# Attention stages of an encoder trunk in another order between its projections: a query tile every four projection steps, first stages begun fewer steps behind their projection

## The chip, the cores and the metric

The kernel runs on one core of a Trainium2 chip. The core has a matrix engine (TensorE, PE in the profile, with its weight loads as PEld), a vector engine (DVE), a scalar engine (ACT), GpSimd (POOL) and a queue that issues the DMAs (SyncE, SP). Each engine works through its own instructions in a fixed order and waits on semaphores for the others. The metric is the device time of one execution in microseconds (us); lower is better. Several executions are timed, and one more is taken with a profile.

## The reference

Two layers of an encoder on 512 tokens of width 1024, all in float32. One layer:

```
h = RMSNorm(x);  z = h @ W_in          # one wide projection, cut into parts
a = DifferentialAttention(z)           # 4 heads; per head two softmaxes p0, p1 over all 512 keys
b = DilatedWindowAttention(z)          # 3 groups x 8 heads, masked windows, joined by denominators
m = (sigmoid(gA) * (a @ W_a) + sigmoid(gB) * (b @ W_b)) @ W_out
x = x + RMSNorm(m);  x = x + RMSNorm(SwiGLU(RMSNorm(x)))
```

Differential attention, per head, with 128-wide values, is

```
s_c = q_c k_c^T / 8;  p_c = softmax(s_c) for c = 0, 1
a = p_0 - lam * p_1;  o = RMSNorm(a @ v) * (1 - lambda_init)
```

Queries and keys pass a rotary embedding (rope) first.

## The kernel before

**Split numbers.** Each large product takes three matmuls: both operands are split into a high and a low part, and high·high, high·low and low·high are added (`mm3`, lines 117 to 123). The high part of a weight is cast on ACT (L106 or L109), the low part is the difference, on DVE (L107 or L110). Rotated queries and keys of differential attention, and of the first dilated group, are split in the same way (L458 on ACT, L459 on DVE).

**Projections are cut into steps.** `ws_gen` (line 191) yields after every 12 matmuls of 128x512, and the value projection `proj_v` yields after 24 of 128x256. Such a stretch of PE work is called a projection step here. `drive` (line 183) runs a projection and calls `att_step` after each step. One layer has 104 steps: 4 for the first half of differential attention (u = 0; its queries and keys were projected earlier), 12 for its second half (u = 1), 72 for the six dilated groups (u = 0, 1; gi = 0, 1, 2) with 12 each, and 16 for gates.

**Attention is a queue of jobs.** `att_push` (line 164) appends a job with the step at which it is due: the clock plus an entry of `DELAY`. `att_step` (line 167) advances the job at the head of the queue by one step, and the job behind it too once the head "drains", that is, once it has begun its last query tile's scores and one period has passed. Thus a job starts when it is due or when the one ahead drains, whichever is later. What the stages of a step issue on PE stands between two projection steps. When the projections end, a loop (`while attq`) empties the queue.

**A job of differential attention** (`da_attn`, line 478) handles two heads and four query tiles of 128 rows. Each tile has four stages: *scores* (24 small matmuls, L484, into four PSUM tiles `at0` to `at3`; then for each head two maxima on DVE, L490, two exponentials on ACT, L492, a reciprocal and two combinations on DVE, L496, L498, L500), *turn* (four PE transposes per head, L510, into `at0` and `at1`, copied out by ACT, L512), *values* (16 matmuls, L519, into `at4`; then squares on ACT, L525, and the norm on DVE and POOL, ending in L530) and *finish* (two transposes, L537, into the upper half of the same `at4`, read by ACT, L540, and DVE, L541). `pipeline` (line 546) sets at which step of the job each stage of each tile runs: stage lag plus period times tile. Before, the period is 3 and the lags are 0, 2, 4 and 6.

**A job of a dilated group** (`g_attn`, line 571) has scores (L583), a masked softmax (L591, L593, L596), a turn (16 transposes, L610, into `at0` to `at3`, copied by DVE, L611) and values (L626 or L629, into `at4`), with a period of 4. Group 0 has two blocks of queries, the others one. **The join** of the three groups (`combine`, line 650) does vector work, lets five steps pass, and then turns its result in two parts (L679, both in `at4`, read by ACT, L682, and DVE, L683).

**Who orders what.** PE's instructions go in the order in which the program writes them. The instructions of the other engines and the DMAs on SP are put in order ahead of the run by a planner, by priority and expected readiness; the splits of weights have a raised priority (`SPLIT_PRI`). Each engine then keeps that order. The buffers of the attention are few: one PSUM tile for each of `at0` to `at4`, three for projections (`pj`), eight tiles `e` for exponentials and what is made of them.

## Time and profile before

| what | value |
|---|---|
| median of 3 runs | 1914.05 us (1913.56 to 1915.93) |
| the profiled execution's own time | 1916.6 us |
| its span, first to last instruction | 1914.8 us |
| PE busy | 1847.7 us, 10720 matmuls |
| DVE busy | 917.0 us |
| ACT busy | 659.3 us |
| POOL busy | 183.0 us |
| mean granted clock of PE | 0.988 |

The profile gives the busy time of each engine, groups of instructions by source line with the idle time before them and who ended it, and the same for stretches of time. A row such as "PE at L510 <- DVE e L500: 9.4, 6, 2.9" reads: PE, at line 510 with output `at`, waited for DVE's line 500 with output `e`; 9.4 us in all, 6 times, 2.9 us the longest. In a row of the timeline, the first number is the start in us from the span's start, the second the duration, and a bracket holds the idle time of the engine just before and what ended it. In a table by stretches, each engine's busy time is followed by its number of instructions; PEclk is the granted clock of PE as a share of full speed. Differential attention lies at about 77 to 215 us in the first layer and 1020 to 1160 us in the second.

### The profile page before, as it was taken

What the parts mean: (1) busy time and instruction counts of PE and PEld (TensorE: products, weight loads), DVE (VectorE), ACT (ScalarE), POOL (GpSimd) and SP (SyncE); (2) the same over time, 40 slices, a digit from 0 to 9 for tenths busy, and PEclk for the clock granted to TensorE, in tenths of its full rate; (3) what the DMA queues carried; (4) which work ended last, traced back from release to release, by engine and by line L of the source; (5) the groups of instructions that cost most, each with busy time, mean ns of one, the idle gap of its engine ahead of it and who ended that gap; (6) DMA issues with size and microseconds to landing.
All of it is one profiled execution on the core that took longest, in us unless ns stands there. A gap on an engine that the chain in (4) does not pass through costs nothing. (4 is left out here: it accounts for less than half of the span.)

```text
span 1914.8 us, 25447 instructions
## 1 busy us (share of the span) xinstructions
PE 1847.7 (96%) x10720; PEld 1579.5 (82%) x10720; DVE 917.0 (48%) x1243; ACT 659.3 (34%) x1273; POOL 183.0 (10%) x132
## 2 busy tenths in 40 slices
PE   6998999999999999999999889999999999999997
PEld 6887888987888888888888779989878888888886
DVE  4565658644446333332455666584443543333222
ACT  3354434443224222221333544333432342222221
POOL 1211113110100000000011111221110000000000
PEclk9998999999999999999999999999999999999999
DMA  6312223222245322323432212232224433232232
GB/s 184 97 45 75 67 90 113 73 88 87 90 150 169 110 88 97 101 88 109 144 115 81 82 45 71 86 117 76 82 88 141 145 111 110 88 102 97 88 121 66
DMA packets 148066, 190.45 MB, mean 99 GB/s; under 512 B 7536, under 2 KB 132848, under 8 KB 147952
## 3 DMA queue, kind: packets, MB, share of 16 engines
q1 hardware_dynamic: 147952, 188.83, 30.8%
q8 instruction: 84, 1.38, 0.3%
q14 instruction: 30, 0.25, 0.0%
HBM read 176.16 MB, written 12.65 MB: 99 GB/s over the span
## 5 line engine op out<-in xcount | busy, mean ns | idle before, releaser
L121 PE MATMUL pj<-hTh,whi 128*128 128x512 f32 (+1 forms) x1536 | 588.7, 383 | 2.5 <-ACT hTh L246 2.5
L122 PE MATMUL pj<-hTl,whi 128*128 128x512 f32 (+1 forms) x1536 | 582.0, 379 | 5.9 <-DVE hTl L247 5.9
L123 PE MATMUL pj<-hTh,wlo 128*128 128x512 f32 (+1 forms) x1536 | 580.7, 378 | 0.0
L107 DVE TENSOR_TENSOR wlo<-raw,whi 128x1024 fp32r<-128x1024 f32 x252 | 338.8, 1345 | 500.5 <-ACT whi L106 500.3
L106 ACT CAST whi<-raw 128x1024 fp32r<-128x1024 f32 x252 | 264.7, 1051 | 772.2 <-PE pj L122 527.5
L121 PEld LDWEIGHTS pj<-hTh,whi 128*128 128x128 f32 x1536 | 292.4, 190 | 60.3 <-ACT hTh L246 4.7
L122 PEld LDWEIGHTS pj<-hTl,whi 128*128 128x128 f32 x1536 | 292.4, 190 | 57.4 <-DVE hTl L247 7.4
L123 PEld LDWEIGHTS pj<-hTh,wlo 128*128 128x128 f32 x1536 | 292.2, 190 | 53.6
L121 PE MATMUL pj<-whi,hTh 128*128 128x256 f32 x512 | 150.3, 294 | 0.0
L122 PE MATMUL pj<-wlo,hTh 128*128 128x256 f32 x512 | 147.2, 288 | 0.0
L123 PE MATMUL pj<-whi,hTl 128*128 128x256 f32 x512 | 147.1, 287 | 0.0
L75 POOL TENSOR_TENSOR sm<-sm,mhalf 128x1 f32<-128x1 f32 (+1 forms) x48 | 30.6, 637 | 1010.0 <-DVE sm L73 1010.0
L121 PEld LDWEIGHTS pj<-whi,hTh 128*128 128x128 f32 x512 | 100.6, 197 | 3.4 <-issue 2.7
L596 ACT ACTIVATE e<-e,gst 128x128 f32<-128x128 f32 (+1 forms) x192 | 81.3, 425 | 58.8 <-DVE gst L593 58.8
L122 PEld LDWEIGHTS pj<-wlo,hTh 128*128 128x128 f32 x512 | 100.8, 197 | 0.2
L123 PEld LDWEIGHTS pj<-whi,hTl 128*128 128x128 f32 x512 | 100.6, 196 | 0.0
L794 DVE TENSOR_TENSOR s<-s,pj 128x512 f32<-128x512 f32 x42 | 28.9, 688 | 123.6 <-PE pj L123 123.6
L285 PE MATMUL at<-whi,ac 128*128 128x512 f32 x200 | 78.8, 394 | 0.0
L284 PE MATMUL at<-whi,ac 128*128 128x512 f32 x200 | 78.5, 392 | 0.0
L286 PE MATMUL at<-wlo,ac 128*128 128x512 f32 x200 | 77.7, 389 | 0.0
L492 ACT ACTIVATE e<-at,sm 128x512 f32<-128x512 f32 x64 | 43.7, 685 | 55.7 <-DVE sm L490 55.7
L110 DVE SCALAR_TENSOR_TENSOR wlo<-raw,whi 128x1024 fp32r<-128x1024 f32 x32 | 48.0, 1503 | 15.6 <-ACT whi L109 15.3
(174 smaller groups left out, 2391.2 us busy)
## 6 DMA issues: line engine op xcount, KB each, us to landing
raw<-in_w_in_dram SPq DMA_DIRECT2D x64, 1024.0 KB, 5.7
raw<-in_w_gate_up_dram SPq DMA_DIRECT2D x44, 1024.0 KB, 5.0
raw<-in_w_down_dram SPq DMA_DIRECT2D x22, 1024.0 KB, 4.9
raw<-in_w_out_dram SPq DMA_DIRECT2D x8, 1024.0 KB, 4.9
xs<-m SPq DMA_DIRECT2D x12, 512.0 KB, 2.9
m<-xs SPq DMA_DIRECT2D x12, 512.0 KB, 5.6
m<-in_x_dram SPq DMA_DIRECT2D x32, 128.0 KB, 5.4
raw<-in_w_a_dram SPq DMA_DIRECT2D x8, 512.0 KB, 3.5
```

Source lines behind the costliest of these rows:

```text
L75: nc.gpsimd.tensor_tensor(out=r, in0=t, in1=mhalf[:, 0:n], op=ALU.pow)
L106: nc.scalar.copy(out=shp(hi), in_=src)
L107: nc.vector.tensor_tensor(out=shp(lo), in0=src, in1=shp(hi.bitcast(F32)), op=ALU.subtract)
L110: nc.vector.scalar_tensor_tensor(out=shp(lo), in0=src, scalar=scale, in1=shp(hi.bitcast(F32)), op0=ALU.mult, op1=ALU.subtract)
L121: nc.tensor.matmul(o, ah, bh, start=(i == 0), stop=False)
L122: nc.tensor.matmul(o, ah, bl, start=False, stop=False)
L123: nc.tensor.matmul(o, al, bh, start=False, stop=(i == n - 1))
L284: nc.tensor.matmul(o, ah, hi[:, sl], start=(k == 0), stop=False)
L285: nc.tensor.matmul(o, al, hi[:, sl], start=False, stop=False)
L286: nc.tensor.matmul(o, ah, lo[:, sl], start=False, stop=(k == nk - 1))
L492: nc.scalar.activation(out=e, in_=oc, func=AF.Exp, bias=nmx[:, c:c + 1], accum_out=den[:, c:c + 1])
L596: nc.scalar.activation(out=e[:, i, :], in_=e[:, i, :], func=AF.Exp, bias=sts[:, n, h:h + 1], accum_out=sts[:, n, 4 + h:5 + h])
```

## The change

```diff
-DELAY = (4, 4, 2, 2, 3)
+DELAY = (1, 3, 1, 1, 2)
...
-            yield from pipeline(NT, 3, ((finish, 6), (values, 4), (turn, 2), (scores, 0)))
+            yield from pipeline(NT, 4, ((turn, 3), (finish, 7), (values, 5), (scores, 0)))
...
             for pr in range(2):
                 yield True
+                yield True
                 tp = at(4, (P, 4, P))
```

No computation is added or removed; only the places of the stages between the projection steps change. `DELAY` holds, in order, the delays of differential attention, of dilated groups 0, 1 and 2, and what is added for u = 0 of differential attention. So the job of u = 0 is due 3 steps after its projection and not 7, that of u = 1 after 1 and not 4, and the groups after 3, 1 and 1 steps and not 4, 2 and 2. Within a job of differential attention a tile's scores come every 4 steps and not every 3. A tile's turn follows its scores 3 steps later and not 2; values follow the turn after 2 steps and finish follows values after 2 steps, as before. In the step that holds a turn and the previous tile's finish, the turn now stands first. In `combine`, one more step passes ahead of each of the two turns.

## Prediction

> **What bounds the kernel now.** I read the page first, then PE's waits, then the stretches around them, then single rows. The page's busy times say that PE is the bound.

> ```profile
> PE 1847.7 (96%) x10720; PEld 1579.5 (82%) x10720; DVE 917.0 (48%) x1243; ACT 659.3 (34%) x1273; POOL 183.0 (10%) x132
> ```

> Of the span of 1914.8 us PE is idle for 67.1, and an order alone can win only from that, and from what the clock loses. PE's waits say where in attention the idle time lies (line, who ended it: us in all, times, longest).

> ```profile
> PE at L510 <- DVE e L500: 9.4, 6, 2.9
> PE at L519 <- DVE big L541: 9.4, 4, 3.7
> PE at L510 <- ACT e L492: 8.5, 4, 2.2
> PE at L679 <- DVE big L683: 4.6, 2, 2.3
> PE at L510 <- DVE sm L73: 2.6, 4, 0.8
> ```

> L510 is the turn: it waits 20.5 us for the softmax of its own tile. L519 is values: it waits for the readers of the last finish, which share `at4`. Both belong to differential attention. L679 is the second turn of the join. The stretches of differential attention, one for each layer, and inside the first one those after long waits:

> ```profile
> 77.00:215.00 138.00, 122.89 (x869) 104.02 (x868) 87.44 (x171) 62.39 (x155) 21.56 (x17) 0.93 0.19 58
> 1020.00:1160.00 140.00, 124.19 (x923) 105.58 (x926) 91.11 (x177) 62.70 (x156) 21.88 (x18) 0.95 0.20 61
> 88.00:93.00 5.00, 4.85 (x28) 4.81 (x28) 1.23 (x2) 1.12 (x2) 0.00 (x0) 0.66 0.39 130
> 132.00:142.00 10.00, 9.28 (x59) 7.56 (x60) 4.88 (x13) 4.14 (x12) 0.70 (x1) 0.66 0.01 2
> 158.00:165.00 7.00, 6.64 (x26) 6.04 (x27) 2.91 (x9) 0.81 (x4) 0.69 (x1) 0.58 0.00 0
> 182.00:187.00 5.00, 4.73 (x22) 3.91 (x26) 3.33 (x9) 1.69 (x4) 0.70 (x1) 0.77 0.00 0
> 195.00:200.00 5.00, 3.33 (x46) 2.54 (x48) 3.35 (x8) 1.17 (x2) 3.11 (x3) 1.00 0.72 210
> 455.00:461.00 6.00, 3.68 (x21) 2.90 (x20) 2.52 (x3) 3.66 (x5) 0.00 (x0) 1.00 0.30 75
> ```

> The first number after the stretch is its length, the second PE's busy time, the third from the end PEclk. PE is idle for 138.00 - 122.89 = 15.1 us in the first layer and 15.8 us in the second. The waits cost again behind them: the granted clock is 0.58 to 0.77 in the four slow stretches. Busy time times missing clock there is 4.85 x 0.34 + 9.28 x 0.34 + 6.64 x 0.42 + 4.73 x 0.23 = 8.7 us. In the second layer the clock misses 0.05 x 140 = 7.0 us against 0.07 x 138 = 9.7; in that ratio I estimate 6.3 us of slow work there. So waits and slow clock of differential attention cost about 15.1 + 8.7 + 15.8 + 6.3 = **45.9 us**. That is the most that its new order can win.

> Which waits they are, in the first layer:

> ```profile
> 88.15 0.63 PE L510 MATMUL at<-ident,e 128*128 128x128 f32 x4 [2.91 <-DVE e L500]
> 131.32 0.63 PE L510 MATMUL at<-ident,e 128*128 128x128 f32 x4 [2.04 <-ACT e L492]
> 132.72 0.73 PE L510 MATMUL at<-ident,e 128*128 128x128 f32 x4 [0.76 <-DVE sm L73]
> 158.36 0.79 PE L519 MATMUL at<-m,e 128*128 128x128 f32 x2 [3.71 <-DVE big L541]
> 180.88 1.08 PE L510 MATMUL at<-ident,e 128*128 128x128 f32 x4 [2.23 <-ACT e L492]
> 197.69 0.63 PE L510 MATMUL at<-ident,e 128*128 128x128 f32 x4 [1.31 <-DVE e L500]
> 199.00 0.51 PE L583 MATMUL at<-op,op 32*128 32x256 f32 x8 [0.37 <-ACT e L512]
> ```

> The slow stretches stand behind waits of 2.91, 2.04 and 0.76 together, 3.71, and 2.23 us. Behind 1.31 us (195 to 200), and behind the join's wait (455 to 461), the clock is 1.00.

> **The change part by part.** How long a step is, and what a tile's stages take on PE:

> ```profile
> 106.23 1.67 PE L484 MATMUL at<-op,op 32*128 32x512 f32 x24
> ...
> 110.70 1.95 PE L519 MATMUL at<-m,e 128*128 128x128 f32 x16
> 112.41 0.48 PE L121 MATMUL pj<-hTh,whi 128*128 128x512 f32 x1
> ...
> 115.25 0.60 PE L510 MATMUL at<-ident,e 128*128 128x128 f32 x4
> ```

> A projection step takes 115.25 - 112.41 = 2.84 us, values 112.41 - 110.70 = 1.71 us, scores at most 1.67 us.

> *A turn one step later.* Between a tile's scores and its turn there were two steps and the last tile's values, 2 x 2.84 + 1.71 = 7.4 us; now three steps, 10.2 us (5.7 and 8.5 us for a first tile). How long the softmax takes is in DVE's rows, here of the tile turned at 131.32:

> ```profile
> 125.64 1.23 DVE L459 TENSOR_TENSOR op<-r,op 128x1024 fp32r<-128x1024 f32 x1 [1.93 <-ACT op L458]
> 126.78 1.28 DVE L490 TENSOR_REDUCE sm<-at 128x1 f32<-128x512 f32 x2
> ...
> 131.82 0.75 DVE L500 SCALAR_TENSOR_TENSOR e<-e,sm,e 128x512 f32<-128x512 f32 x1
> ```

> Once begun it takes 131.82 + 0.75 - 126.78 = 5.8 us, and fits even the old gap. But it began late: DVE idled 1.93 us at the head of its queue, for the cast of a rope's result on ACT, with the maxima behind it. Of the four turns quoted above, the step of 2.84 us leaves 0.1 of the wait of 2.91 and nothing of 2.04 + 0.76, 2.23 and 1.31. Tiles now meet other ropes and splits, so I don't take zero: between 0 (covered) and 1.0 us (a third of the old worst) for each of the 16 tiles, I take 0.25, near the covered end, since all four land there. That leaves **4 us**.

> *Values two steps behind finish.* The 3.71 us came where the last finish of one job and the first values of the next stood in one step, with nothing between. Now that tile's finish is followed by the next job's scores (1.6 us) and a step: 4.4 us of cover. Within a job it is two steps and scores, not one. The nearest price is that of 3.71, so I take 0; the other end is half a us each, 2 us in all.

> *Scores straight behind a turn.* Where one job drains into the next, a turn and the next job's scores still share a step, and the scores need `at0` and `at1` back. The row at 199.00 has that, 0.37 us. A finish of two small transposes now stands between them, but no slow clock hides a part any more. Two places in a layer at 0.5 us leave **2 us**; bounds 0 and 3.

> *A new wait.* Group 1's delay falls from 2 to 1, and group 0's job comes later because the queue is longer. By the rules of the queue, for u = 0: the first job starts at step 7 (due 3 behind 4), drains at its 16th and lets the second start at 22, that one drains at 37 and lets group 0 start, whose second turn is its eighth step, 44, where it drains. Group 1 was pushed at 40 and is due at 41, so its scores come in step 44 too. Before, the starts were 11, 22 and 33, group 0's second turn came at 40, and group 1 was due at 42. That turn writes `at0` to `at3`, which DVE copies out, and the scores need all four. When PE went on behind the same turn before, and when its copies ran:

> ```profile
> 233.04 0.47 PE L121 MATMUL pj<-hTh,whi 128*128 128x512 f32 x1
> ```

> ```profile
> 232.24 0.68 DVE L611 COPY e<-at 128x512 f32<-128x512 f32 x1
> 232.84 1.22 DVE L107 TENSOR_TENSOR wlo<-raw,whi 128x1024 fp32r<-128x1024 f32 x1
> 233.97 1.88 DVE L611 COPY e<-at 128x512 f32<-128x512 f32 x3
> ```

> PE could go on at 233.04, the copies end at 233.97 + 1.88 = 235.85: a wait of 2.8 us; without the split of a weight between them, 1.6. I take 2.3, and 0.7 for a slow clock in half the cases: 3.0 us in each layer, **6 us**. Bounds 3 and 9. Queued behind the scores on PE is the projection, so nothing hides it.

> [...]

> *The join.* For u = 0 a step more stands between its two turns, which had no wait. For u = 1 the queue runs out: its first turn falls into the last attention step behind the gates, the second into the loop that follows, before (104, 105) and after (104, 106). The added step there holds no PE work, and the 4.6 us stay: **0**.

> *What else moves.* Only the first job starts really earlier, at step 7 and not 11. The second starts at 22 in both, since the first drains then; the later groups shift by -1 to +4 steps. The first job's scores come at about 77 - 4 x 2.84 = 66 us, behind the split of its keys (first row below). In u = 1, group 0's scores come one step sooner behind their query's rope:

> ```profile
> 54.73 1.22 DVE L459 TENSOR_TENSOR op<-r,op 128x1024 fp32r<-128x1024 f32 x1 [2.92 <-ACT op L458]
> ...
> 322.70 1.22 DVE L459 TENSOR_TENSOR op<-r,op 128x1024 fp32r<-128x1024 f32 x1 [2.27 <-ACT op L458]
> ...
> 328.12 1.70 PE L583 MATMUL at<-op,op 32*128 32x256 f32 x48
> ```

> They had 328.12 - 323.92 = 4.2 us to spare and lose 2.84 and a turn of 0.5: still 0.8. I take 0; bound 2 us. Every DMA keeps its kind and size. On SP the rearranging moves of group 0 go up to four steps later past the weight loads; the join that needs them is 14 steps off.

> *The sum.* -45.9 + 4 + 2 + 6 = **-33.9 us**. From the profiled 1916.6 that gives 1882.7; the runs' median lies 2.5 us below the profiled execution, so 1914.05 - 33.9 = **1880 us**, 1.8% faster.

> **The rivals.** *Everything hides.* The planner finds an order in which turns and the new wait cost little: 1914 - 45.9 = 1868 to 1872 us. For: DVE is busy 87.44 of 138 us, so there is room. Against: a turn and scores share a step in three places.

> *DVE's order keeps the turns late.* As at 125.64, an instruction that waits for POOL and ACT stands ahead of the maxima. Tiles start more often just ahead of a rope than before. With 1.0 us of wait and 0.6 us of slow clock for each of 16 tiles, 25.6 us and not 4: 1902 us. Against: a step of 2.84 us is more than every such delay quoted except 2.91.

> *Slower: the chain outgrows its cover.* The same queue, but at every tile. It costs from 10.2 us on; at 12.8 us a tile waits 2.6 us, and with 1.4 us of slow clock 16 tiles pay 64 us. With the 8 us of the other terms that exceeds 45.9 by 26: 1940 us. It turns slower than before above 45.9 - 8 = 38 us, 2.4 us for each tile, that is a chain of about 11.8 us. For: the tile turned at 131.32 had its second head ready 7.4 + (132.72 - 131.32) + 2.04 = 10.8 us behind its scores. Against: of the first layer's eight tiles only two were near that (the turns at 131.32 and 180.88), and the same DVE work is now spread over more steps. [...]

> *It doesn't do what it says.* The starts are set by the queue and not by `DELAY` from the second job on, and if the planner merely follows PE, each wait moves along: about 1914 us. Against it stands that the period itself changes.

> **How the numbers follow.** The forecast (1872 to 1890) has 0.55, everything hidden 0.13, late turns (1890 to 1908) 0.20, no change 0.04, slower 0.08. The range is 1868 to 1903: it holds the first two and most of the third. What this kernel's measurement can tell from no change is about 0.2%, 4 us. Faster by more than that has 0.55 + 0.13 + 0.20 = 0.88, within it 0.04, slower 0.08.

> **What would show it.** L519's wait for L541 is gone; L510's waits fall from 20.5 to about 4 us; the clock of the differential stretches rises from 0.93 and 0.95 to 0.98 or more; L583 waits about 2 us for L611 once in each layer; L679 keeps 4.6 us. PE's busy time falls by 10 to 15 us though its work is the same. I am wrong if L510 still waits over 12 us, or if projection lines wait for `pj` or for weights, which they don't now.

## The result, and the profile after

The changed kernel takes 1885.15 us (median of 4 runs, 1884.36 to 1885.48) against 1914.76 us (4 runs, 1913.56 to 1915.93): 0.9845 of the time before, 95% interval 0.9828 to 0.9862, or 29.6 us less. Measured again on another chip it is 0.9839 (0.9823 to 0.9854). The prediction was 1880 us, 33.9 us less than before. The profiled execution took 1885.48 us, with a span of 1883.7 us and a mean granted clock of 0.993 (before 0.988). Of all executions in this document one took 5277 us, of the kernel begun at step 10; it counts in that kernel's median in the table below, but not in its ratio.

The page's busy times of the changed kernel, and PE's waits (line, who ended it: us in all, times, longest):

```profile
PE 1839.2 (98%) x10720; PEld 1572.7 (83%) x10720; DVE 916.4 (49%) x1243; ACT 656.9 (35%) x1273; POOL 176.2 (9%) x132
```

```profile
PE at L680 <- DVE big L684: 4.7, 2, 2.3
PE at L583 <- DVE e L611: 3.7, 4, 1.7
PE at L484 <- ACT e L512: 2.3, 2, 1.1
PE at L510 <- DVE e L500: 0.8, 2, 0.4
PE at L610 <- ACT e L596: 0.4, 2, 0.2
```

L519, 9.4 us before, is gone from the list. L510, 20.5 us before, is down to 0.8. The join keeps what it had (now L680, one line further down). New are 3.7 us of L583 waiting for DVE's copies, and 2.3 us of L484. PE's busy time falls by 8.5 us with the same 10720 matmuls: they ran at a higher clock (0.993 against 0.988). By stretches (length, PE's busy time, and PEclk third from the end), the two layers' differential attention, and in the first layer the 3.6 us at the end of the new wait:

```profile
66.00:215.00 149.00, 147.28 (x1117) 127.77 (x1116) 106.08 (x195) 73.38 (x180) 27.06 (x20) 1.00 0.25 74
1009.00:1160.00 151.00, 147.78 (x1150) 129.08 (x1143) 104.52 (x193) 70.18 (x182) 26.20 (x20) 0.99 0.25 73
224.10:227.70 3.60, 3.53 (x58) 3.41 (x58) 0.74 (x3) 0.00 (x0) 1.28 (x1) 0.53 0.86 262
```

Idle time of PE in the first layer's stretch is 149.00 - 147.28 = 1.7 us where it was 15.1, in the second 3.2 (the new wait stands inside it) where it was 15.8; the clock is 1.00 and 0.99 where it was 0.93 and 0.95. The slow place left in attention besides the join (last section) is the new wait. On PE's timeline (start, duration, instruction, and in brackets the idle time before it), and DVE's rows there:

```profile
219.00 1.91 PE L610 MATMUL at<-ident,e 128*128 128x128 f32 x16
220.84 0.48 PE L583 MATMUL at<-op,op 32*128 32x128 f32 x2
222.97 4.80 PE L583 MATMUL at<-op,op 32*128 32x128 f32 x62 [1.65 <-DVE e L611]
227.71 0.50 PE L121 MATMUL pj<-hTh,whi 128*128 128x512 f32 x1
```

```profile
219.81 0.68 DVE L611 COPY e<-at 128x512 f32<-128x512 f32 x1
220.40 1.92 DVE L107 TENSOR_TENSOR wlo<-raw,whi 128x1024 fp32r<-128x1024 f32 x1
222.24 1.87 DVE L611 COPY e<-at 128x512 f32<-128x512 f32 x3
```

The place and the mechanism are those of the prediction: group 0's second turn (L610) and group 1's scores (L583) share a step, and between DVE's four copies stands the split of a weight, 1.92 us. The block of scores lasts 227.71 - 220.84 = 6.87 us, and 6.93 us in the second layer (from 1149.02 to 1155.95). Undisturbed, in the kernel before, it lasted 244.20 - 242.20 = 2.00 us:

```profile
242.20 2.07 PE L583 MATMUL at<-op,op 32*128 32x128 f32 x64
244.20 0.50 PE L121 MATMUL pj<-hTh,whi 128*128 128x512 f32 x1
```

So the new wait costs 4.9 us a layer. The profile calls only 1.65 us of it a wait, but PE waits longer: two matmuls start at 222.97, two at 223.57 and the next at 224.17, each time when DVE has copied one more of the four tiles, and the last copy ends at 222.24 + 1.87 = 224.11. In between, the profile counts the few matmuls as busy. Only then do the rest run, and at a granted clock of 0.53 (the last row by stretches). What the wait costs without a slow clock is seen in the second layer of the kernel with the pipeline line alone (next section), where the same place has a clock of 1.00:

```profile
1155.79 0.48 PE L583 MATMUL at<-op,op 32*128 32x128 f32 x2
1157.92 3.24 PE L583 MATMUL at<-op,op 32*128 32x128 f32 x62 [1.65 <-DVE e L611]
1161.10 0.38 PE L121 MATMUL pj<-whi,hTh 128*128 128x256 f32 x1
```

```profile
1159.10:1162.70 3.60, 3.58 (x71) 3.46 (x72) 2.26 (x4) 0.00 (x0) 1.27 (x1) 1.00 0.86 266
```

That block lasts 1161.10 - 1155.79 = 5.31 us, 3.3 more than the undisturbed 2.00. So 3.3 us a layer are the wait itself, and 6.87 - 5.31 = 1.6 us are the slow clock (1.6 in the second layer too).

### The profile page after: what moved, and what is told of

Its sections match the earlier page's. It is cut to its first block, busy times and chain, and to the rows that moved or that the text cites. A ratio compares the mean times of both kernels' runs of the same rounds, so it can differ in the third digit from the quotient of the medians.

```text
span 1883.7 us, 25452 instructions
## 1 busy us (share of the span) xinstructions
PE 1839.2 (98%) x10720; PEld 1572.7 (83%) x10720; DVE 916.4 (49%) x1243; ACT 656.9 (35%) x1273; POOL 176.2 (9%) x132
## 5 line engine op out<-in xcount | busy, mean ns | idle before, releaser
L121 PE MATMUL pj<-hTh,whi 128*128 128x512 f32 (+1 forms) x1536 | 587.7, 383 | 3.2 <-ACT hTh L246 3.2
L107 DVE TENSOR_TENSOR wlo<-raw,whi 128x1024 fp32r<-128x1024 f32 x252 | 338.1, 1342 | 479.7 <-ACT whi L106 479.4
L106 ACT CAST whi<-raw 128x1024 fp32r<-128x1024 f32 x252 | 264.8, 1051 | 741.0 <-PE pj L122 499.2
L121 PEld LDWEIGHTS pj<-hTh,whi 128*128 128x128 f32 x1536 | 291.4, 190 | 61.5 <-ACT hTh L246 5.4
L121 PE MATMUL pj<-whi,hTh 128*128 128x256 f32 x512 | 147.0, 287 | 0.0
L596 ACT ACTIVATE e<-e,gst 128x128 f32<-128x128 f32 (+1 forms) x192 | 81.5, 426 | 91.0 <-DVE gst L593 91.0
L121 PEld LDWEIGHTS pj<-whi,hTh 128*128 128x128 f32 x512 | 98.1, 192 | 2.0 <-issue 1.4
L492 ACT ACTIVATE e<-at,sm 128x512 f32<-128x512 f32 x64 | 43.8, 687 | 65.5 <-DVE sm L490 65.5
L591 DVE TENSOR_TENSOR e<-at,mk 128x512 f32<-128x512 f32 x64 | 41.1, 684 | 35.6 <-PE at L583 35.6
```

The costliest lines, as they stand in the source:

```text
L106: nc.scalar.copy(out=shp(hi), in_=src)
L107: nc.vector.tensor_tensor(out=shp(lo), in0=src, in1=shp(hi.bitcast(F32)), op=ALU.subtract)
L121: nc.tensor.matmul(o, ah, bh, start=(i == 0), stop=False)
L492: nc.scalar.activation(out=e, in_=oc, func=AF.Exp, bias=nmx[:, c:c + 1], accum_out=den[:, c:c + 1])
L591: nc.vector.tensor_tensor(out=e, in0=o[h], in1=mask, op=ALU.add)
L596: nc.scalar.activation(out=e[:, i, :], in_=e[:, i, :], func=AF.Exp, bias=sts[:, n, h:h + 1], accum_out=sts[:, n, 4 + h:5 + h])
```

## The experiments

My theory after the result: the pipeline line alone takes away the waits of differential attention; the shorter delays bring little, and what they bring is spent on the new wait and on the added step of the join. The rival: the delays bring much of it themselves.

| kernel | us, median | of before | 95% interval |
|---|---|---|---|
| changed kernel, measured again | 1884.72 | 0.9839 | 0.9823 to 0.9854 |
| pipeline line alone | 1880.08 | 0.9808 | 0.9794 to 0.9821 |
| delays alone | 1887.00 | 0.9844 | 0.9831 to 0.9858 |
| changed, join step undone | 1876.40 | 0.9790 | 0.9777 to 0.9804 |
| changed, group 1 later | 1874.47 | 0.9785 | 0.9772 to 0.9799 |
| changed, turn lag 2 | 1894.17 | 0.9886 | 0.9870 to 0.9901 |
| old period, start at step 8 | 1896.79 | 0.9904 | 0.9890 to 0.9917 |
| old period, start at step 10 | 1884.81 | 0.9830 | 0.9814 to 0.9845 |
| pipeline line, later drain, shorter join | 1871.80 | 0.9769 | 0.9756 to 0.9782 |
| pipeline line, groups 1 and 2 later, shorter join | 1868.95 | 0.9758 | 0.9743 to 0.9773 |
| changed, both costs out | 1867.35 | 0.9750 | 0.9733 to 0.9767 |

**The pipeline line alone.** The kernel before with this edit, `DELAY` and the join as they were:

```diff
-            yield from pipeline(NT, 3, ((finish, 6), (values, 4), (turn, 2), (scores, 0)))
+            yield from pipeline(NT, 4, ((turn, 3), (finish, 7), (values, 5), (scores, 0)))
```

> The kernel before with the pipeline line alone changed (period 4, turn 3 steps behind its scores); delays and join as before. My theory: the pipeline line brings nearly the whole gain of differential attention, whenever the first job begins. Then PE's waits at L510 and L519 fall from 29.9 us to under 4, and the median lands at 1885 plus or minus 4 us. By the rules of the queue group 0's second turn and group 1's scores share a step here too (48), so PE waits for L611 again, about 1.9 us a layer with a slow clock behind it. Rival: the earlier start of the first job (step 7, not 11) is needed to spread DVE's work; then L510 keeps 8 us or more and the median lies at 1893 to 1905.

Measured: 1880.08 us, 0.9808, just below the expected 1881 to 1889. PE's waits in attention:

```profile
PE at L679 <- DVE big L683: 4.6, 2, 2.3
PE at L583 <- DVE e L611: 3.3, 2, 1.6
PE at L484 <- ACT e L512: 0.6, 2, 0.3
```

L510 and L519 are both gone: the longer period and the third step are enough for all of differential attention. It is also faster than the whole change, by some 6 us: 0.9808 against 0.9839 and 0.9845. (The kernel before took 1914.87 to 1916.41 us on three of the chips, and so these are compared as ratios to it on the same chip.) The other two edits together cost time. By the rows, L484 waits 1.7 us less here than in the changed kernel, L510 0.8 and the second halves (L583 and L610) 0.8, and the two blocks of the new wait are 1.7 us shorter: 5.0 of the 5.4 us between the two spans. And the wait of L583 comes with the longer period, not with `DELAY`: group 0 starts later, and its second turn falls into the step in which group 1 begins.

**The delays alone.**

```diff
-DELAY = (4, 4, 2, 2, 3)
+DELAY = (1, 3, 1, 1, 2)
```

> The kernel before with the delays alone changed; period 3 and the join as before. My theory: differential attention keeps its waits (L510 15 to 25 us, L519 7 to 11 us), since its stages stand as close as before. The join gains something that the whole change gave away: its two turns come at steps 103 and 104, with a projection step of 2.84 us between them, so its wait of 4.6 us goes. Median 1904 to 1914 us, best guess 1909. Rival: starting earlier takes work off DVE where the turns wait; median under 1900.

Measured: 1887.00 us, 0.9844. That misses the expectation by 17 us or more and lies in the rival's band: the delays alone bring about as much as the whole change. PE's waits:

```profile
PE at L510 <- DVE e L500: 9.4, 4, 3.1
PE at L519 <- DVE big L541: 5.8, 2, 2.9
...
PE at L510 <- DVE sm L73: 0.4, 2, 0.2
```

L510 waits 9.8 us and not 20.5, though a turn has its old two steps. The join's wait is gone. The two edits of the change are two remedies for the same waits, and don't add. Why the old period waits less with an earlier start was open. Two theories: the *early start* itself (more of the softmax before DVE fills up), or the *phase*: with a period of three, the scores of a tile stand at other distances from the end of a rope's projection when the first job starts at step 7 than when it starts at step 11.

**Start at steps 8 and 10, old period.** The kernel before with

```diff
-DELAY = (4, 4, 2, 2, 3)
+DELAY = (1, 3, 1, 1, 3)     # first job due at step 8
...
+DELAY = (1, 3, 1, 1, 5)     # the other kernel: at step 10
```

> The kernel with the delays alone changed, and its first job begun one step later still (step 8 and not 7; before it was 11); period 3. It asks why the delays alone won 29 us. Theory of phase: what counts is where a tile's scores stand to the end of a rope's projection (steps 7, 11, 19, 27, 31). At a start of 8 the scores come at 8, 11, 14, 17, 19, 22, 25, 28: the first and the last right behind such an end, 11 and 19 one step ahead of one, so L510 waits 16 to 25 us again; with the join's wait gone 1900 to 1910 us. Theory of an early start: less DVE work where the turns wait, three steps of four are kept: L510 under 12 us, 1886 to 1892.

> As the one before, but begun at step 10, one step earlier than the kernel before. Phase: the scores come at 10, 13, 16, 19, 21, 24, 27, 30; only 19 and 27 stand one step ahead of the end of a rope's projection, none right behind one: L510 waits 5 to 10 us, and the median is 1884 to 1892. Early start: one step of four alone, so most of the waits of before stay: L510 14 to 20 us, 1900 to 1910.

> The same kernel as the one with starts at step 10 and the old period, for its trace. Theory, that a turn of the old period waits where its scores stand a step ahead of or right behind a rope: L510 waits no more than 10 us in all, as in the kernel with DELAY alone (9.8), against 19 with starts at step 8 and 20.5 before. Rival, that the early start and not the phase decides: 14 us or more. 1880 to 1888 us.

Measured: start at 8, 1896.79 us; at 10, 1884.81 us, and 1883.35 us (0.9833, 0.9810 to 0.9856) in the repeat, whose trace is used here. PE's waits at the turn, start at 8, then start at 10:

```profile
PE at L510 <- ACT e L492: 12.2, 4, 3.9
PE at L510 <- DVE e L500: 5.4, 8, 1.2
PE at L510 <- DVE sm L73: 1.5, 2, 0.8
```

```profile
PE at L510 <- DVE e L500: 7.6, 6, 1.6
PE at L510 <- ACT e L492: 1.6, 2, 0.8
```

By start step, L510 waits 9.8 us (7), 19.1 (8), 9.2 (10) and 20.5 (11, the kernel before). Starts three steps apart agree and neighbours differ by a factor of two, so it isn't how early the job starts, and the phase fits. It fits tile by tile too. In the first layers of the four kernels the theory names twelve tiles, those whose scores stand right ahead of or right behind a rope's end: steps 7 and 27 (start 7), 8, 11, 19 and 28 (start 8), 19 and 27 (start 10), and 11, 20, 28 and 31 (start 11). Eleven of them wait 1.1 to 4.3 us at their turn, and step 19 of start 8 not at all; of the twenty others one waits 1.6 us (step 10 of start 10) and the rest 0.5 us or less. (The time at start 8 lay between what the two theories expected, since the earlier start takes away the join's wait too; the wait of L510 tells them apart.) The rows of the first tile at start 8 show what the phase does, on PE, DVE and ACT:

```profile
67.14 1.67 PE L484 MATMUL at<-op,op 32*128 32x512 f32 x24
78.34 1.04 PE L510 MATMUL at<-ident,e 128*128 128x128 f32 x4 [3.90 <-ACT e L492]
```

```profile
72.72 1.23 DVE L459 TENSOR_TENSOR op<-r,op 128x1024 fp32r<-128x1024 f32 x1 [2.27 <-ACT op L458]
73.86 1.28 DVE L490 TENSOR_REDUCE sm<-at 128x1 f32<-128x512 f32 x2
```

```profile
71.64 1.05 ACT L458 CAST op<-r 128x1024 fp32r<-128x1024 f32 x1 [3.57 <-POOL r L420]
```

The scores end at 67.14 + 1.67 = 68.8, and their first maximum starts at 73.86: five us late. Ahead of it in DVE's order stands the split of a rope (L459), which waits for ACT's cast (L458), which waits for POOL (L420). That the rope at the head of the queue is the cause is read from these rows and from those at 125.64 in the prediction. A kernel in which the planner puts the maxima ahead of the rope was not tried.

**The changed kernel with the old turn lag.** Period 4, but the turn two steps behind the scores:

```diff
-            yield from pipeline(NT, 4, ((turn, 3), (finish, 7), (values, 5), (scores, 0)))
+            yield from pipeline(NT, 4, ((turn, 2), (finish, 7), (values, 5), (scores, 0)))
```

> The changed kernel with the turn 2 steps behind its scores again and not 3; period 4 and all else as changed. It asks whether the extra step is what covers the softmax. Theory: a turn waits when its scores stand right ahead of, or right behind, the end of a rope's projection and the gap is only two steps and values (7.4 us, 5.7 for a first tile). Here the scores of steps 7, 11 and 19 stand one step ahead of such an end (7, 11, 19), so these three wait, 3.0, 1.5 to 3 and 1.5 to 3 us in each layer; L510 waits 12 to 18 us in all and the clock slows behind some: 1897 to 1908 us. Rival: at period 4 DVE has room enough and the lag does not matter: 1884 to 1888.

Measured: 1894.17 us, 0.9886. PE's waits at the turn:

```profile
PE at L510 <- DVE e L500: 11.4, 6, 3.1
PE at L510 <- DVE sm L73: 1.5, 2, 0.8
```

12.9 us against 0.8 with the third step. The three tiles that the expectation names do wait, 3.1, 1.1 and 1.5 us in the first layer, and one more waits 0.8. The time lies 3 us below the theory's band and above the rival's. The cover is then the old 7.4 us, and spreading the tiles over more steps does not suffice: the third step between scores and turn is what takes the waits away. In ratios it is worth 0.9886 - 0.9839, 9 us. The waits at the turn differ by 12.1 us; 2.3 us of that the changed kernel gives back at L484, which doesn't wait here. That leaves 9.8 us; the slow clocks, which differ between the two kernels as well, were not added up. L519 does not wait here either, so its wait goes with the longer period or with the new order of turn and finish, and these two were not separated.

**The two costs of the change, one by one and together.** The changed kernel without the added step of the join; with group 1 begun four steps later; and with both:

```diff
             for pr in range(2):
                 yield True
-                yield True
...
-DELAY = (1, 3, 1, 1, 2)
+DELAY = (1, 3, 5, 1, 2)
```

> The changed kernel without the added step in the join. The two turns of the second join then come at steps 103 and 104 and not at 104 and 106, so one projection step of 2.84 us lies between them. My theory: the wait of 4.7 us for L684 in the changed kernel goes, and with it the 1.5 us of slow clock behind it in one layer: median 1885 - 5 to 6 = 1879 to 1880 us. Rival: the added step is neutral, since the readers of the first turn are held by other work on ACT and DVE and not by time: 1885 plus or minus 1.

> The changed kernel with group 1's delay at 5 and not 1, so that its scores come one step behind group 0's second turn (45 and 44) and not in the same step. My theory: the pair cost 6.87 us in the first layer and 6.94 us in the second where undisturbed scores take 2.0, so 9.8 us go, waits and slow clock together: median about 1875 us, waits for L611 under 0.6 us. If only the idle time of 3.8 us were the cost, and the slow clock had another cause, about 1881. Rival: the wait moves to group 1's own turn or values, which come later in both halves: 1882 to 1886.

> The changed kernel with both single undos together: the join's added step left out, and group 1 begun four steps later. Each alone gained 9.7 and 10.9 us of span. Theory, that the two terms (scores behind group 0's second turn, and the join's turn past the end of the queue) are separate: they add, span 1863 and time 1864 to 1867 us, and PE's waits hold neither L583 nor the join, while the 2.3 us at L484 for ACT stay. Rival, that each single undo also gained from a clock which varies between kernels: the rows of the two places hold only 9.8 and 6.3 us, so 1867 to 1871 us.

Measured: 1876.40, 1874.47 and 1867.35 us. The first is 3 us below its theory, the second is where its theory had it. PE's waits in attention, in this order:

```profile
PE at L583 <- DVE e L611: 3.3, 2, 1.7
PE at L484 <- ACT e L512: 2.3, 2, 1.1
```

```profile
PE at L680 <- DVE big L684: 4.7, 2, 2.3
...
PE at L583 <- DVE e L611: 0.4, 2, 0.2
```

```profile
PE at L484 <- ACT e L512: 2.3, 2, 1.1
PE at L510 <- DVE e L500: 0.8, 2, 0.4
```

Each edit removes the wait it is aimed at, and besides it 0.4 us or so of other waits (L583 in the first, L610 in the second). The first is the more telling: with the new delays both turns of the second join fall inside the queue (steps 103 and 104) and wait for nothing; the added step pushes them to 104 and 106, one past the end of the projections, and the wait of 2.3 us a layer is back. Both together give 0.9750 against 0.9839 for the changed kernel on the same chip, about 17 us. The single gains, from ratios to before, are 9.4 and 10.3 us, 20 in all. The rows alone hold 9.8 us for the new wait, and 4.7 us for the join with 1.5 us for the slow clock behind it. The result lies at the border of the two expectations, and its runs (1865.3 to 1869.9) reach into both. The profiles show something that belongs to neither edit: at the end of the first layer, from 946 to 952 us, far from both, the changed kernel has a granted clock of 0.72 and its repeat too, and so has the kernel with both costs out at 936 to 942 us. Neither single undo has a slow clock there (1.00 from 936 to 956 us). The missing clock is worth about 4.71 x 0.28 = 1.3 us in the changed kernel (busy time times missing clock) and 1.4 to 1.5 us in the other two, so each single gain holds that much which its edit isn't shown to cause. That is 2.6 to 3 us for the two, about as much as the sum of the single gains, 20, exceeds the 17 of both together. This rests on one profiled execution of each kernel.

> The changed kernel itself beside its variants on one chip. If the period alone is worth more than the whole change, it stays at 0.983 to 0.986 of before, above the 0.9808 of the period alone; if that difference came from the chip, it lands at 0.980 to 0.982.

The changed kernel beside it: 0.9839, inside the first of the two bands. So the pipeline line alone is better than the whole change on this measure too.

**Versions that close the gaps from the other side.** The kernel before with the new pipeline line, and one of

```diff
# first version: the queue is told of the drain one step later, the join waits 3 steps
-                yield j >= n * period - 1
+                yield j >= n * period
-            for _ in range(5):
+            for _ in range(3):
# second version: groups 1 and 2 later, the join waits 2 steps
-DELAY = (4, 4, 2, 2, 3)
+DELAY = (4, 4, 9, 4, 3)
-            for _ in range(5):
+            for _ in range(2):
```

> The kernel before with the pipeline line as changed, the delays as before, a job's drain told one step later (so that the next job's scores never share a step with a turn), and the join's five empty steps cut to three (its second turn then comes at step 103 and has a projection step ahead of it and behind it). Theory: against the pipeline line alone (1880.1 us where before was 1916.4) the pair of scores behind group 0's turn (4.8 and 3.3 us), the two other pairs (1.0 and 0.8 us a layer) and the join (2.9 and 3.0 us) go: 1880 - 17.5 = 1862 to 1864 us, 0.972 of before. Rival: the later starts of the second job put its scores one step ahead of three rope ends, and turns wait again: 1868 to 1878.

> The kernel before with the new pipeline line, and with the two places closed where the period-only kernel still loses: group 1 is begun five steps late (9 in DELAY), so its scores stand one step behind group 0's second turn and not in the same step, and the join is told to wait 2 steps and not 5, so that both its turns stand inside the queue. By the rows of the period-only kernel the scores behind the turn lose 4.8 and 3.3 us (wait and slow clock behind it) and the join 2.9 and 3.0 us. Theory, that these are lost time and nothing takes their place: 1880.1 - 8.1 - 5.9 = 1866 us (1864 to 1868), L583 and the join wait no more. Rival, that closing them moves later jobs onto ropes and onto other readers, as in the kernel with all gaps closed, where the second values of group 1 waited 2.0 us in each layer: 1869 to 1873 us, with a new line of PE's waits of 3 to 5 us.

Measured: 1871.80 and 1868.95 us. (The second edit also begins group 2 later, with a delay of 4 and not 2, which its expectation doesn't mention.) The first is some 8 us above its theory and inside its rival's band, though not for the rival's reason, since no turn waits; the second lies between its theory and its rival, 2.9 us above the theory's 1866. PE's waits, first version, then second:

```profile
PE at L629 <- ACT m L630: 4.0, 2, 2.0
PE at L537 <- DVE e L530: 3.4, 6, 0.7
```

```profile
PE at L629 <- ACT m L630: 2.9, 2, 1.4
```

L583 and the join no longer wait, and in their place a group's second values (L629) wait for ACT to copy the first out of the same `at4`. In the first version this is group 1, whose copy on ACT stands behind the exponentials of group 2 (L596, from 260.6 to 267.7 us in the first layer); with the 3.4 us of L537 its waits come to 7.4 us, and the clock is slow behind L629 (0.59 and 0.57 over 4 us). In the second version it is group 2, begun later by the edit (scores at 265.29 us, second values at 287.78), and the copy stands behind the cast of a weight (L106); that wait, 2.9 us, is as large as what is missing from the 1866 us expected. Group 2 with its old delay was not tried here. All three of the best kernels lie within 0.2% of each other, at 0.975 to 0.977 of before.

## Why the prediction was right, and where it was off

**Waits and slow clock of differential attention, 45.9 us: right.** Of the 30.9 us idle in the two stretches 4.9 are left, 1.9 of them in the new wait, and the clock there is 1.00 and 0.99. The pipeline line alone does this, as the prediction had it. What the prediction didn't see is that the delays alone do half of it at the turns. It took the start of the first job, four steps earlier, as an edit at nothing ("the later groups shift by -1 to +4 steps") and never asked how the phase of tiles and ropes changes; with the old period that is worth some 10 us of L510's wait. With the new period and the third step no kernel's turns waited over 0.4 us, wherever its jobs began, so the omission did not hurt the sum. (Those starts cover only two of the four places a period of four has; the others weren't tried.)

**Turns left, 4 us: too much.** 0.8 us of waiting is left, at the first tile of each layer. The choice "near the covered end" was right, and even 0.25 us a tile was more than came. The rival "DVE's order keeps the turns late" has its mechanism (the rope ahead of the maxima is there), but a third step covers it; with two steps and the same spread it costs the 12.9 us of the run above.

**Scores straight behind a turn, 2 us: the size held, the place didn't.** L484 waits 2.3 us, but not in the step shared by two jobs. It is the third tile of the second job, one step behind the turn of the tile ahead. ACT's and PE's rows:

```profile
157.20 1.05 ACT L458 CAST op<-r 128x1024 fp32r<-128x1024 f32 x1 [5.25 <-POOL r L420]
158.15 1.07 ACT L512 COPY e<-at 128x512 f32<-128x512 f32 x2
```

```profile
158.79 2.15 PE L484 MATMUL at<-op,op 32*128 32x512 f32 x24 [1.13 <-ACT e L512]
```

ACT's copies of the turn stand behind a rope's cast that waits 5.25 us for POOL, and PE's scores need the copied tiles back. It is the fault of the old turns once more, one consumer further on.

**The new wait, 6 us: the step that was mis-sized.** Its step, its partners and its mechanism were right; both of its sizes were too small. The wait itself was put at 2.3 us and costs 3.3: counted as the prediction counted it, from PE's arrival to the end of the last copy, it is 224.11 - 220.84 = 3.3 us, and the weight's split between the copies took 1.92 us and not 1.22. The slow clock was put at 0.7 us a layer, for "a slow clock in half the cases", and costs 1.6 us in each layer. By the same reckoning (a block's length less 5.31 us) it costs 0.6 to 1.6 us in eight of the ten blocks of the five profiles that have this wait, and nothing in two. The prediction's bound of 9 us for both layers was passed: it was 9.8.

**The join, 0: right as a sum, wrong in its parts.** The 4.6 us stayed. But the delays alone would have taken them away, and the added step brought them back: two edits that cancel, where the prediction had one without effect. That its sum came out at 0 is luck. It counted the steps of the changed kernel only (104 and 106) and not those without the added step (103 and 104).

**The sum.** Predicted -33.9 us, measured -29.6 by medians and 1885.48 - 1916.6 = -31.1 between the profiled executions. The new wait took 3.8 us more, waits of 0.2 us at L583 and L610 in the second halves 0.8 us, and a slow clock behind the join in one layer 1.5 us (last section); the turns took 3.2 us less. That leaves -33.9 + 3.8 + 0.8 + 1.5 - 3.2 = -31.0, near the difference of the profiled executions. Errors of both signs are in it, 6.1 us too little cost and 3.2 us too much, and that the sum came within 3 to 4 us is partly luck. PE's busy time fell by 8.5 us and not by 10 to 15 because PE counts as busy for some 3 us more in each block of the new wait (4.99 and 5.05 us, 2.00 undisturbed).

The rival "slower", a chain that outgrows its cover at every tile, had nothing in any kernel with three steps.

## What to carry to other kernels

When a stage sits behind an in-order queue that also serves another chain, look at where the stage falls against that chain before adding slack: here a shift of one step at the old period halved the waits or doubled them, and one more step of slack removed them. Cost a change of several edits against each of them alone; two that cancel look like one that does nothing, and here one of the best kernels is the change with two of its own side effects removed. A wait on TensorE should be priced with the slow clock that may follow it, here up to 1.6 us behind the new wait of 3.3 us. And it should be measured by what the block takes and not by the idle time alone, which here showed 1.88 us of those 3.3, since a few matmuls between the pieces of a wait count as busy.

## What was not expected of the hardware

The same wait is followed by a slow clock in some places and not in others. The join's second turn waits 2.32 to 2.33 us in six of the profiles (the kernel before, the changed one and its repeat, and three variants), twice in each, with the same instructions behind it. Changed kernel, first and second layer, on PE:

```profile
441.17 0.66 PE L680 MATMUL at<-ident,m 128*128 128x128 f32 x4 [2.33 <-DVE big L684]
...
442.67 0.63 PE L122 MATMUL pj<-big,whi 128*128 128x512 f32 x1
443.10 0.63 PE L123 MATMUL pj<-big,wlo 128*128 128x512 f32 x1
...
1369.41 0.66 PE L680 MATMUL at<-ident,m 128*128 128x128 f32 x4 [2.33 <-DVE big L684]
```

In the first layer the matmuls start 0.43 us apart from 442.67 on, and from 446.01 on 0.23 us again; in the second layer no such stretch follows (16 matmuls are in the last row below, 10 in the first layer's second row). The slow stretch begins 1.5 us after PE has resumed and lasts 3.3 us. Eight matmuls run in it that would have taken 8 x 0.23 = 1.84 us, so it costs 1.5 us. The granted clock in the 4 us behind this wait, by layer, is 1.00 and 1.00 in the kernel before, 0.57 and 1.00 in the changed one, 1.00 and 0.57 in its repeat, 0.68 and 0.72 with the pipeline line alone, 0.71 and 1.00 with group 1 later, 0.57 and 1.00 with turn lag 2: six of twelve are slow.

```profile
439.10:442.51 3.41, 1.34 (x8) 1.20 (x9) 1.85 (x3) 2.77 (x5) 0.00 (x0) 1.00 0.20 58
442.51:445.92 3.41, 3.41 (x10) 2.62 (x9) 0.67 (x1) 0.00 (x0) 0.00 (x0) 0.50 0.81 248
```

```profile
1367.52:1370.93 3.41, 1.52 (x9) 1.34 (x10) 2.04 (x3) 2.59 (x4) 0.00 (x0) 1.00 0.25 62
1370.93:1374.34 3.41, 3.41 (x16) 2.72 (x15) 1.17 (x2) 0.00 (x0) 0.00 (x0) 1.00 0.78 246
```

In the first layer PE is idle for 3.41 - 1.34 = 2.07 us of the window, and the next is slow; in the second for 1.89 us, and the next is not. Over all twelve waits of the join, the largest piece in one window is 2.07 to 2.33 us in the six that are followed by a slow clock and 1.21 to 1.89 us in the six that are not (1.21 and 1.71 us in the kernel before). So whether this wait costs 1.5 us more goes with where it falls in the grid. The border, between 1.89 and 2.07 us, was worked out for this wait alone; no run moved a wait within the grid to test it.

Behind the new wait the clock isn't always slow either: in eight of ten blocks (above).
